# Two value projections of a hybrid decoder layer as one product of seven block products, ahead of the token mixer

## Chip, cores and metric

One Trainium2 chip, one of its cores. The metric is the device time of one execution in microseconds, the median of several runs.

## What is computed

A trunk of two layers on 1024 tokens of 1024 channels. The first layer mixes tokens by gated DeltaNet and short convolutions, the second by HGRN2 (4 heads) and by dilated sliding-window attention (3 dilations, 4 heads); each is followed by a SwiGLU feed-forward part. The change is in the second layer's input projection, whose columns are split into seven parts:

```python
hq, hf, hi, hg, sq, sk, sv = split_cols(h @ w_in, CD_SPLITS)   # 512 x 4, 1536 x 3 columns
o_c = hgrn2_recurrence(heads(silu(hq)), heads(k_in), heads(hi), heads(log_f))
for p, (window, dilation) in enumerate(((128, 1), (512, 4), (2048, 16))):
    o_p, lse_p = dilated_window_attention(sq[:, :, p], sk[:, :, p], sv[:, :, p], window, dilation)
```

`hi` are the values of HGRN2 (512 columns), `sv[:, :, 1]` those of dilation 4 (512 columns). Inside a head, HGRN2 is a recurrence over chunks of the sequence; attention gives an output and a log-sum per dilation, and the three are combined by a softmax.

## The kernel before, in words

Every product of the projections is done in three terms: operands are split into a high and a low half (`split`, line 100: a cast on ScalarE, a subtraction on VectorE), and `mm3` (line 125) sends high x high, high x low and low x high, its three matmuls at lines 135, 136 and 137. A weight unit is 128 x 1024 and has four slots; the raw weights come through a buffer `raw` with two slots and a `spare` with one. PSUM has eight banks: `psu` (3), `psm` (3), `psg` (2).

`Up` (line 288) and its subclass `Local` (line 752) work a pair of projections as one 2 x 2 block product with seven products in place of eight. Its operands are the four quarters of the normalized input, b11 and b21 (first half of the tokens, low and high channels), b12 and b22 (second half), and four combinations t1 to t4 of them. `Local.run` makes queries, keys and HGRN2's inputs this way, f = 0 to 15, and writes them to DRAM. Its instructions on TensorE, VectorE, ScalarE, GpSimd and, from f = 3, the SP queue are in an order written out by hand (`manual_schedule`). In the last pair it loads two weight units for the next stage and takes b12 back from DRAM into the place of t1. In the feed-forward part, `Up.pair` also makes, on VectorE, sums of blocks of the down weights (`block_load`, `block_sums`, lines 457 to 473), 256 columns at a time, and stores them to DRAM.

`mixer_cd` (line 1970) then mixes. Its values are plain products: `v_rows` for HGRN2, two heads (256 columns) at a time, eight token tiles by eight k tiles by three terms; `swa_v(p)` for a dilation, 512 columns. Between groups of their matmuls `tick(cost)` adds credit, rate x cost, to two generators and runs as many of their steps as there is credit for (saved up to 3): `hg_chain`, the recurrence (eight units of head and half, ten steps each, rate 2.2), and `loc`, the attention (three dilations by four heads by four steps, rate 1.6, in the gates 2.5). So value products, and last the gates of HGRN2 (`hgrn_gates`), are what TensorE does while the vector engines work on the two chains. The order is: values of heads 0 and 1, of dilation 4, of heads 2 and 3, of dilation 16, of dilation 1, the gates. The chain may not pass the heads whose values are there (`have_v`). Values of HGRN2 stay in SBUF (`vt`), those of the dilations go through DRAM (`scr_v`). In `mixer_cd` the order on the engines is chosen when the program is built, by the order in which the code issues.

Of the kernel before, what the change touches and what calls it, by code (L numbers as in the profile page):

```python
# [9 lines left out]
F32 = mybir.dt.float32  # L10
# [21 lines left out]
PAIRS = [(None, h) for h in range(4)] + [(p, h) for p in (1, 2, 0) for h in range(4)]  # L32
VGROUPS = ((8, 2), (10, 2), (40, 4), (44, 4), (48, 4))

# [21 lines left out]
def hybrid_trunk_kernel(ctx: ExitStack, tc: tile.TileContext, x_t, w_all, w_down, w_ba, vecs, c_f, c_i, c_rope, out):  # L56
# [97 lines left out]
    hd = [[dr.tile([P, KT, HT], F32, name=f"hd{j}{i}") for i in range(NH)] for j in range(3)]  # L154
    cat = [[dr.tile([KT, P, HT], F32, name=f"cat{i}{j}") for j in range(NH)] for i in range(2)]

    class Trunk:
# [130 lines left out]
    class Up:  # L288
# [168 lines left out]
        def block_load(self):  # L457
            if self.blocks < ND // SB:
                c = slice(self.blocks * SB, (self.blocks + 1) * SB)
                a = self.right.tile([P, 4, SB], F32, tag="sd", name="sd", bufs=1)  # L460
                dma(a, w_down[self.layer].rearrange("x y p n -> p (x y) n")[:, :, c])
                self.block = c, a
                self.blocks += 1

        def block_sums(self):
            if self.block:
                c, a = self.block
                V.tensor_tensor(a[:, 3], a[:, 2], a[:, 3], op=ADD)
                V.tensor_tensor(a[:, 2], a[:, 0], a[:, 2], op=SUB)
                V.tensor_tensor(a[:, 0], a[:, 3], a[:, 0], op=SUB)  # L470
                V.tensor_tensor(a[:, 1], a[:, 1], a[:, 0], op=SUB)
                dma(self.sums_d.rearrange("s p n -> p s n")[:, :, c], a)
                self.block = None
# [20 lines left out]
        def pair(self, f, b11, b21, b22, t1, t2, t3, t4):  # L494

            n = f + 1
            self.p1(f, b11)
            self.add22(f - 1)
# [27 lines left out]
            self.end12(f - 1, b22)  # L526
            if f in (5, 7, 9, 11):
                self.block_sums()
# [3 lines left out]
            self.p6(f, t2)  # L532
            if f in (5, 7, 9, 11):
                self.block_load()
# [217 lines left out]
    class Local(Up):  # L752
# [185 lines left out]
        def run(self, tr, row, b11, b21, hx, close, left, right):  # L938
# [7 lines left out]
            with tc.manual_schedule(engines=engines | {E.SP}):  # L946
                last = len(PAIRS) - 1
                for f in range(3, last + 1):
                    self.pair(f, f == last, b11, b21, b22, t1, t2, t3, t4)
                self.copy22(last)  # L950
                self.add22(last)
                self.end21(last, t4)
                self.rope22(last)
                split(self.lead_w[1][:, 0, :], self.lead_w[1][:, 1, :], self.lead_raw)
                for i, raw in enumerate(self.back):
                    c = slice(2 * i, 2 * i + 2)
                    split(t1[0][:, c, :], t1[1][:, c, :], raw.rearrange("p (k t) -> p k t", k=2))
                self.end12(last, b22)
                self.rope21(last)
                self.add12(last)  # L960
                self.rope12(last)
                while self.adds or self.stores:
                    self.flush()
            return [t1, b22], self.lead_w

        def pair(self, f, last, b11, b21, b22, t1, t2, t3, t4):
# [6 lines left out]
            if not last:  # L973
                an = self.raw("g", n, n % 3 == 1)
            else:
                raws = [self.left.tile([P, DM], F32, tag="spare", name="raw", bufs=1),
                        ring.tile([P, DM], F32, tag="raw", name="raw", bufs=2)]
                for raw, j in zip(raws, (8, 9)):
                    dma(raw, w_all[W_AT["cd", j]])
            self.add22(f - 1)  # L980
# [26 lines left out]
            if last:  # L1007
                self.lead_w = [unit(), unit()]
                split(self.lead_w[0][:, 0, :], self.lead_w[0][:, 1, :], raws[0])
                self.lead_raw = raws[1]  # L1010
            self.rope12(f - 1)
            if not last:
                self.s = self.sums(an, bn)
                self.a, self.b = an, bn
            else:
                self.back = [ring.tile([P, DM], F32, tag="raw", name="raw", bufs=2) for _ in range(2)]
                for i, raw in enumerate(self.back):
                    dma(raw.rearrange("p (k t) -> p k t", k=2), self.b12[:, 2 * i:2 * i + 2, :])
            if f == 3:
# [950 lines left out]
    def mixer_cd(hn, hp, qkd, wv):  # L1970
        catd = cat[1]
        scr_v = dr.tile([3, T_LEN, HT], F32, name="scr_v")
        scr_o = dr.tile([4, 2, T_LEN, 132], F32, name="scr_o")
# [3 lines left out]
        with ExitStack() as es:  # L1977
# [9 lines left out]

            def v_rows(w, tick, dst, tts=range(8)):

                v = [u.rearrange("p z (k e) -> p z k e", k=KH) for u in w]  # L1990
                for tt in tts:
                    half, j = divmod(tt, 4)
                    o = psu()
                    t = slice(j * P, (j + 1) * P)
                    mm3(o[:, 0:256], [(hk(hn[half], 0, k)[:, t], hk(hn[half], 1, k)[:, t], v[k // KH][:, 0, k % KH],
                                       v[k // KH][:, 1, k % KH]) for k in range(KT)])
                    dst(tt, o[:, 0:256])
                    tick(0.5)

            wp = es.enter_context(pool("swa", side="right"))
            attn = hl("attn", (4, P))
            G.memset(attn, 0.0)
            st, carry = hl("st", (3, P)), hl("carry", (P,))
            vts, raws = {}, {}

            def hgrn_v(pair, w, tick, tts=range(8)):
                def put(tt, o):
                    half, j = divmod(tt, 4)  # L2010
                    if j == 0:
                        while pair and half and done_c[0] < 3:
                            next(hg_chain)
                        vts[pair, half] = hl("vt", (4, 256), 3)
                    S.copy(vts[pair, half][:, j, :], o)
                v_rows(w, tick, put, tts)

            def hgrn_vw(pair):
                return wload(("cd", 8 + pair * 2), ("cd", 9 + pair * 2))

# [5 lines left out]
            def hgrn_fq(h, half):  # L2026
                raws[h, half] = [hl(n, bufs=2) for n in ("b", "kk", "q")]
                for i, z in zip((2, 3, 1), raws[h, half]):
                    dma(z, qkd[None, h][i, :, half * HT:(half + 1) * HT])

            def hgrn(h, half, states):
                if half + h == 0:
                    hgrn_fq(0, 0)
                b, kk, q = raws.pop((h, half))
                if h * 2 + half < 7:
# [90 lines left out]
                yield  # L2126
                vt = vts[h // 2, half]
                hv = slice(h % 2 * P, h % 2 * P + P)
                last = half == NH - 1
                o = psg()  # L2130
                for c in range(4 - last):
                    T.matmul(o[:, c * P:(c + 1) * P], kt[:, c, :], vt[:, c, hv], start=True, stop=True)
                before = [states.get(h)] + [st[:, c, :] for c in range(3)]
# [12 lines left out]
                for c in range(4):  # L2146
                    T.matmul(po[:, c * P:(c + 1) * P], attn[:, c, :], vt[:, c, hv],
                             start=True, stop=before[c] is None)
# [37 lines left out]

            def swa_v(p, tick):


                w = wload(*(("cd", 40 + p * 4 + i) for i in range(4)))  # L2190
                v = [u.rearrange("p z (k e) -> p z k e", k=2) for u in w]
# [220 lines left out]

            done_c, have_v, diag = [0], [0], []
            gate_store = [None]
# [4 lines left out]
            def chain():  # L2419
                states = {}  # L2420
                for u in range(8):
                    h, half = divmod(u, 2)
                    while have_v[0] <= h // 2:
                        yield
                    yield from hgrn(h, half, states)
# [34 lines left out]
            hg_chain, loc = chain(), local()  # L2460
            credit, rate = [0.0, 0.0], [2.2, 1.6]

            def tick(cost):

                live = have_v[0] * 4 > done_c[0], bool(wanted or heads or busy[0])
                for i in range(2):
                    credit[i] = min(credit[i] + rate[i] * cost, 3.0 if live[i] else 1.0)
                while credit[0] >= 1 and have_v[0] * 4 > done_c[0]:
                    credit[0] -= 1
                    next(hg_chain, None)  # L2470
# [6 lines left out]

            hgrn_v(0, wv, tick, range(4))
            have_v[0] = 1
            hgrn_v(0, wv, tick, range(4, 8))  # L2480
            swa_v(1, tick)
            attend(1)
            w1 = hgrn_vw(1)
            hgrn_v(1, w1, tick, range(4))
            have_v[0] = 2
            hgrn_v(1, w1, tick, range(4, 8))
            swa_v(2, tick)
            attend(2)
# [270 lines left out]
```

## Time and profile before

| | us |
|---|---|
| median of three runs (2511.23 to 2512.3) | 2511.42 |
| the profiled execution | 2512.06 |
| its span | 2509.5 |
| busy: TensorE, VectorE, ScalarE, GpSimd | 2495.7, 1671.8, 1097.2, 626.7 |

The span is from the first to the last instruction of the profiled execution; some 2.6 us of the device time lie around it. Busy times are unions of the instructions of one engine. Matmuls overlap, so the time beside one of them is longer than the distance to the next. In the second mixer the stages are: 1416 to 1448 us the values of heads 0 and 1 (and the rest of the last pair), to 1503 us those of dilation 4, to 1545 us those of heads 2 and 3, to 1617 us those of dilation 16, to 1687 us those of dilation 1, to 1777 us the gates. "DVE" is VectorE, "ACT" ScalarE, "POOL" GpSimd, "PE" TensorE, "SP" the queue that issues the transfers.

### The profile page before, as it was taken

What the parts mean: (1) busy time and instruction counts of PE and PEld (TensorE: products, weight loads), DVE (VectorE), ACT (ScalarE), POOL (GpSimd) and SP (SyncE); (2) the same over time, 40 slices, a digit from 0 to 9 for tenths busy, and PEclk for the clock granted to TensorE, in tenths of its full rate; (3) what the DMA queues carried; (4) which work ended last, traced back from release to release, by engine and by line L of the source; (5) the groups of instructions that cost most, each with busy time, mean ns of one, the idle gap of its engine ahead of it and who ended that gap; (6) DMA issues with size and microseconds to landing.
All of it is one profiled execution on the core that took longest, in us unless ns stands there. A gap on an engine that the chain in (4) does not pass through costs nothing. (4 is left out here: it accounts for less than half of the span.)

```text
span 2509.5 us, 37550 instructions
## 1 busy us (share of the span) xinstructions
PE 2495.7 (99%) x13955; PEld 2077.6 (83%) x13955; DVE 1671.8 (67%) x2773; ACT 1097.2 (44%) x1934; POOL 626.7 (25%) x591
## 2 busy tenths in 40 slices
PE   9999999999999999999999999999999999999998
PEld 7888888888888888888888889888888888888887
DVE  8987775675556565567788766566668555666654
ACT  5432134343333344444676545556544333334442
POOL 1321111323333300031566410000132333330001
PEclk9999999999999999999999999999999999999999
DMA  4535458334556588644344544577733555668753
GB/s 156 164 122 168 137 164 271 102 113 168 185 193 217 202 295 287 198 139 135 129 147 139 172 147 142 157 203 224 257 118 101 186 181 185 217 202 304 266 177 126
DMA packets 281454, 451.48 MB, mean 180 GB/s; under 512 B 49176, under 2 KB 137784, under 8 KB 281016
## 3 DMA queue, kind: packets, MB, share of 16 engines
q1 hardware_dynamic: 280984, 448.57, 54.6%
q8 instruction: 109, 1.79, 0.3%
q10 hardware_dynamic: 288, 0.52, 0.1%
q14 instruction: 73, 0.60, 0.1%
HBM read 304.74 MB, written 144.26 MB: 179 GB/s over the span
## 5 line engine op out<-in xcount | busy, mean ns | idle before, releaser
L103 DVE TENSOR_TENSOR w<-raw,w 128x1024 fp32r<-128x1024 f32 (+1 forms) x327 | 388.2, 1189 | 141.5 <-ACT w L102 140.6
L102 ACT CAST w<-raw 128x1024 fp32r<-128x1024 f32 (+1 forms) x327 | 309.5, 952 | 286.0 <-PE psu L137 145.9
L135 PE MATMUL psu<-hnh,w 128*128 128x512 f32 x772 | 308.5, 400 | 0.0
L137 PE MATMUL psu<-hnh,w 128*128 128x512 f32 x772 | 301.3, 390 | 0.0
L136 PE MATMUL psu<-hnl,w 128*128 128x512 f32 x772 | 301.2, 390 | 0.0
L196 POOL TENSOR_TENSOR acc<-acc,sq 128x512 f32<-128x512 f32 x52 | 78.2, 1504 | 441.3 <-ACT sq L192 441.2
L335 POOL TENSOR_TENSOR ws<-raw 128x512 f32<-128x512 f32 x54 | 70.2, 1299 | 431.8 <-DMA raw<-in_dram 256.5
L135 PEld LDWEIGHTS psu<-hnh,w 128*128 128x128 f32 x772 | 145.1, 188 | 30.8 <-ACT sq L192 0.8
L137 PEld LDWEIGHTS psu<-hnh,w 128*128 128x128 f32 x772 | 144.9, 188 | 30.9
L136 PEld LDWEIGHTS psu<-hnl,w 128*128 128x128 f32 x772 | 145.2, 188 | 28.3
L103 DVE TENSOR_TENSOR w<-ws,w 128x1024 fp32r<-128x1024 f32 x51 | 70.1, 1374 | 117.2 <-ACT w L102 117.2
L103 DVE TENSOR_TENSOR hidq<-hr,hidq 128x1024 fp32r<-128x1024 f32 x72 | 82.3, 1144 | 77.8 <-ACT hidq L102 77.6
L102 ACT CAST hidq<-hr 128x1024 fp32r<-128x1024 f32 x72 | 70.2, 979 | 103.8 <-DMA hr<-ts 63.0
L135 PE MATMUL psm<-hidq,w 128*128 128x512 f32 (+1 forms) x275 | 106.1, 386 | 0.0
L136 PE MATMUL psm<-hidq,w 128*128 128x512 f32 (+1 forms) x275 | 105.8, 385 | 0.0
L137 PE MATMUL psm<-hidq,w 128*128 128x512 f32 (+1 forms) x275 | 105.8, 385 | 0.0
L426 POOL TENSOR_TENSOR hid<-hid,c 128x512 f32<-128x512 f32 x44 | 62.0, 1408 | 170.5 <-ACT hid L425 170.4
L341 POOL TENSOR_TENSOR raw<-raw,ws 128x512 f32<-128x512 f32 x51 | 78.7, 1543 | 60.4 <-DVE w L103 53.0
L135 PE MATMUL psu<-t4h,w 128*128 128x512 f32 x240 | 93.5, 390 | 0.0
L137 PE MATMUL psu<-t4h,w 128*128 128x512 f32 x240 | 93.4, 389 | 0.0
L136 PE MATMUL psu<-t4l,w 128*128 128x512 f32 x240 | 93.4, 389 | 0.0
L135 PE MATMUL psu<-t3h,w 128*128 128x512 f32 x240 | 93.4, 389 | 0.0
(544 smaller groups left out, 6716.1 us busy)
## 6 DMA issues: line engine op xcount, KB each, us to landing
raw<-in_dram SPq DMA_DIRECT2D x225, 512.0 KB, 4.2
sd<-in_dram SPq DMA_DIRECT2D x44, 512.0 KB, 4.2
hid<-hid SPq DMA_DIRECT2D x88, 256.0 KB, 3.1
sd<-sd SPq DMA_DIRECT2D x44, 512.0 KB, 3.3
hr<-ts SPq DMA_DIRECT2D x40, 512.0 KB, 4.4
raw<-sd SPq DMA_DIRECT2D x40, 512.0 KB, 4.5
qk<-z SPq DMA_DIRECT2D x52, 256.0 KB, 3.9
hd<-h SPq DMA_DIRECT2D x48, 256.0 KB, 2.8
```

Of the source, the lines that this page charges most:

```text
L102: S.copy(hi, src)
L103: eng.tensor_tensor(lo, src, hi.bitcast(F32), op=SUB)
L135: T.matmul(o, lh, rh, start=first and i == 0, stop=False, **kw)
L136: T.matmul(o, lh, rl, start=False, stop=False, **kw)
L137: T.matmul(o, ll, rh, start=False, stop=last and i == n - 1, **kw)
L196: (eng or G).tensor_tensor(a, a, q, op=ADD)
L335: G.tensor_tensor(s[:, HT:], b[:, :HT], b[:, HT:], op=ADD)
L341: G.tensor_tensor(a[:, HT:], a[:, HT:], s[:, :HT], op=SUB)
L426: G.tensor_tensor(h, h, self.c22.pop(f), op=MULT)
```

## The change

HGRN2's and dilation 4's values become the left and right half of one 1024 x 1024 by 1024 x 1024 product, done in seven block products on the operands that `Local` has, in a new stage `rows` at the end of its hand-written order:

- `rows` sends 336 matmuls of 512 columns. Four banks `x` are carried through the products of b11, t2, t3 and t4; products of b21, t1 and b22 go to `psm` and are added on VectorE. Results go to DRAM: `scr_v[1]` for dilation 4, a new `scr_v[3]` for HGRN2.
- Its weights are 14 units, two for each product, requested three ahead (`v_ask`) and split (`v_unit`); two more units are for dilation 16. Six are blocks of the weights as they are, eight are sums of four blocks, laid into `vsum` in DRAM.
- These sums are made by eight more steps of `block_load` and `block_sums`, in the pairs of the first layer's feed-forward part: pairs 4 to 15 have two such steps each, where pairs 5, 7, 9 and 11 had.
- b12 is taken back into t1 at the end of `rows`.
- `mixer_cd` has no value products of HGRN2 and of dilation 4. A unit of the chain loads its values (128 x 4 x 128) with its other inputs. Attention of dilation 4 and the chain begin at once, beside the values of dilation 16. The rates are 3.5 and 2.0.

```diff
+VSETS = (8, 10, 44, 46)
+VGROUPS = ((8, 4), (40, 4), (44, 4), (48, 4))
...
         def block_load(self):
+            n = self.blocks - ND // SB
+            if n < (0 if self.layer else 2 * DM // SB):
                 a = self.right.tile([P, 4, SB], F32, tag="sd", name="sd", bufs=1)
...
+                    i, c = n // (DM // SB), slice(n % (DM // SB) * SB, (n % (DM // SB) + 1) * SB)
+                    for j, at in enumerate(VSETS):
+                        dma(a[:, j], w_all[W_AT["cd", at + i]][:, c])
+                    d = vsum[:, i].rearrange("s p n -> p s n")[:, :, c]
...
+            more = (5, 7, 9, 11) if self.layer else range(4, 16)
...
-            if f in (5, 7, 9, 11):
+            if f in more:
                 self.block_sums()
...
+        def v_ask(self):
...
+                blk = (8, 10, 0, 2, 3, 1, 46)[i // 2]
+                src = w_all[W_AT["cd", blk + k]] if blk >= 8 else vsum[blk, k]
...
+        def rows(self, last, b11, b21, b22, t1, t2, t3, t4):
+
+            def prod(o, i, q, j, ks=range(KH), first=False, end=False):
+                t = slice(j * P, (j + 1) * P)
+                mm3(o, [(q[0][:, k, t], q[1][:, k, t], self.vu[i + k // 2][:, 0, k % 2], self.vu[i + k // 2][:, 1, k % 2])
+                        for k in ks], first, end, skip_group_check=True)
...
+            for j in range(4):
+                y.append(psm())
+                prod(y[j], 2, b21, j, first=True, end=True)
+                g.append(zt())
+                S.copy(g[j], x[j])
+                if j > 1:
+                    self.v_unit()
+                    self.v_ask()
+                V.tensor_tensor(g[j], g[j], y[j], op=ADD)
+                store(3, 0, j, g[j])
...
+            for a in (0, 2):
+                z = []
+                for j in (a, a + 1):
+                    z.append(psm())
+                    prod(z[-1], 8, t1, j, first=True)
+                    c = late(j)
+                    V.tensor_tensor(c, c, z[-1], op=ADD)
+                    store(1, 1, j, c)
+                if a == 0:
+                    self.v_unit()
+                    self.v_unit()
+                    self.v_ask()
+                    self.v_ask()
...
+                for i, j in enumerate((a, a + 1)):
+                    prod(z[i], 10, b22, j, end=True)
+                    V.tensor_tensor(u2[j], u2[j], z[i], op=ADD)
+                    store(3, 1, j, u2[j])
+            for j in range(4):
+                prod(x[j], 12, t4, j, end=True)
...
+                vt = hl("vt", (4, P), 2)
+                dma(vt, scr_v[3, half * HT:(half + 1) * HT, h * P:(h + 1) * P].rearrange("(c p) d -> p c d", p=P))
...
-            credit, rate = [0.0, 0.0], [2.2, 1.6]
+            credit, rate = [0.0, 0.0], [3.5, 2.0]
...
-            hgrn_v(0, wv, tick, range(4))
-            have_v[0] = 1
-            hgrn_v(0, wv, tick, range(4, 8))
-            swa_v(1, tick)
             attend(1)
-            w1 = hgrn_vw(1)
-            hgrn_v(1, w1, tick, range(4))
-            have_v[0] = 2
-            hgrn_v(1, w1, tick, range(4, 8))
-            swa_v(2, tick)
+            next(hg_chain)
+            swa_v(2, tick, wv)
             attend(2)
             swa_v(0, tick)
             attend(0)
```

## Rows read from the trace of the kernel before

**Rows 1.** The page, span and busy time of the engines over the whole run.

```profile
span 2509.5 us, 37550 instructions
...
PE 2495.7 (99%) x13955; PEld 2077.6 (83%) x13955; DVE 1671.8 (67%) x2773; ACT 1097.2 (44%) x1934; POOL 626.7 (25%) x591
```

**Rows 2.** Busy time per engine in five stages, 1423 to 1777 us.

```profile
core 0: us, PE busy (x) PEld busy (x) DVE busy (x) ACT busy (x) POOL busy (x), PEclk, DMA share, GB/s
1423.00:1448.00 25.00, 24.65 (x384) 24.14 (x384) 20.88 (x47) 14.94 (x27) 4.20 (x6) 1.00 0.82 285
1448.00:1503.00 55.00, 55.00 (x561) 45.48 (x550) 31.47 (x75) 20.47 (x42) 5.74 (x11) 1.00 0.37 122
...
1545.00:1617.00 72.00, 71.72 (x676) 60.89 (x676) 38.56 (x123) 34.21 (x91) 5.94 (x11) 1.00 0.58 159
1617.00:1687.00 70.00, 68.09 (x820) 56.61 (x807) 44.27 (x168) 37.42 (x117) 6.20 (x12) 1.00 0.68 191
1687.00:1777.00 90.00, 89.38 (x723) 76.39 (x722) 66.20 (x256) 65.83 (x204) 2.15 (x5) 1.00 0.72 220
```

**Rows 3.** What PE waited for, 1423 to 1778 us, the longest.

```profile
PE psm L2309 <- ACT sc L2304: 1.3, 1, 1.3
```

**Rows 4.** Timeline of PE: start us, us, first and last of two unbroken runs.

```profile
1400.01 0.39 PE L135 MATMUL psm<-hnh,w 128*128 128x512 f32 x1
...
1416.10 0.39 PE L137 MATMUL psu<-t3h,w 128*128 128x512 f32 x1
1416.33 0.28 PE L135 MATMUL psu<-w,hnh 128*128 128x256 f32 x1
...
1422.91 0.28 PE L135 MATMUL psu<-w,hnh 128*128 128x256 f32 x1
...
1430.70 0.28 PE L137 MATMUL psu<-w,hnl 128*128 128x256 f32 x1
```

**Rows 5.** Timeline of PE where the output projection begins.

```profile
1778.32 0.47 PE L135 MATMUL psg<-hnh,w 128*128 128x512 f32 x1
```

**Rows 6.** Groups by line and form, PE, 1416.2 to 1778 us.

```profile
L135 PE MATMUL psu<-w,hnh 128*128 128x512 f32 x96 | 39.0, 406 | 0.3 <-ACT sw L2200 0.3
...
L135 PE MATMUL psu<-w,hnh 128*128 128x256 f32 x64 | 18.6, 291 | 0.3 <-ACT vt L2015 0.3
```

**Rows 7.** Groups by line and form, VectorE and ScalarE, 1423 to 1778 us.

```profile
L103 DVE TENSOR_TENSOR w<-raw,w 128x1024 fp32r<-128x1024 f32 x21 | 25.6, 1219 | 6.8 <-ACT w L102 6.7
L102 ACT CAST w<-raw 128x1024 fp32r<-128x1024 f32 x22 | 23.0, 1047 | 23.4 <-PE psu L137 21.3 <-DMA raw<-in_dram 2.1
...
L2200 ACT COPY sw<-psu 128x512 f32<-128x512 f32 x24 | 14.1, 585 | 31.6 <-PE psu L137 21.2 <-issue 5.8 <-PE psm L2326 1.8
...
L2051 DVE TENSOR_TENSOR m<-m,kk 128x256 f32<-128x256 f32 x32 | 13.4, 419 | 7.6 <-ACT m L2050 7.5
```

**Rows 8.** Timeline of VectorE, one 128x512 addition out of PSUM.

```profile
1417.65 0.68 DVE L884 TENSOR_TENSOR psm<-c,psg 128x512 f32<-128x512 f32 x1
```

**Rows 9.** DMA issues by tile, 1416 to 1778 us: count, KB, us to landing.

```profile
raw<-in_dram SPq DMA_DIRECT2D x23, 512.0 KB, 4.8
```

**Rows 10.** Groups by line, VectorE, 500 to 900 us: block sums.

```profile
L469 DVE TENSOR_TENSOR sd<-sd 128x256 f32<-128x256 f32 x22 | 13.7, 624 | 0.8
...
L471 DVE TENSOR_TENSOR sd<-sd 128x256 f32<-128x256 f32 x22 | 12.4, 563 | 0.8
L470 DVE TENSOR_TENSOR sd<-sd 128x256 f32<-128x256 f32 x22 | 12.3, 557 | 0.8
L468 DVE TENSOR_TENSOR sd<-sd 128x256 f32<-128x256 f32 x22 | 10.4, 472 | 7.7 <-issue 3.6 <-DMA sd<-in_dram 3.0 <-DVE w L103 1.0
```

**Rows 11.** Busy time per engine in the first up stage, columns as above.

```profile
500.00:600.00 100.00, 100.00 (x443) 82.81 (x442) 73.12 (x87) 43.32 (x58) 29.79 (x21) 1.00 0.40 133
```

**Rows 12.** Busy time per engine in two short stretches of the second mixer.

```profile
1500.00:1510.00 10.00, 10.00 (x190) 9.19 (x189) 9.74 (x29) 7.43 (x16) 0.70 (x1) 1.00 0.51 161
1660.00:1670.00 10.00, 9.72 (x158) 8.03 (x155) 9.70 (x45) 8.81 (x32) 1.10 (x3) 1.00 0.78 200
```

## What the change was predicted to do, before it was run

> **What bounds the kernel now.** I read four views. The page comes first: TensorE is busy for 2495.7 of the 2509.5 us, VectorE for 67% [rows 1]. Busy is not the same as at its peak, so next come the stages around the change. The granted clock is 1.00 throughout, the 2.4 GHz level, so no part of the sum is a clock. VectorE is at 31.47 of 55.0 us in one stage and at 66.20 of 90.0 us in the last; TensorE has hardly a hole [rows 2]. The list of waits agrees: the longest wait that TensorE shows in the whole second mixer is 1.3 us [rows 3]. Last, the timeline, for what a matmul really takes. The duration printed beside a 128x512 matmul (0.39 us) overlaps the next one, so I take the distance of starts. From 1400.01 to 1416.10 us there are 72 of them one after another, 16.09 / 71 = 0.2266 us each. From 1422.91 to 1430.70 us there are 66 of 256 columns, 7.79 / 65 = 0.1198 us each [rows 4]. Half the columns cost 0.53 of the time, so columns are what is paid for, and the way to shorten this stretch is to send fewer of them. The stretch runs from the first value matmul at 1416.33 us to the first of the output projection at 1778.32 us [rows 4, 5]: 362.0 us.
>
> **Removed.** HGRN2's values are 384 matmuls of 256 columns (L135 has 64 + 32 + 32 of them, L136 and L137 as many), 384 x 0.1198 = 46.0 us. The values of dilation 4 are a third of the 576 of 512 columns that the three dilations send (96 + 48 + 48 for each of three lines) [rows 6]: 192 x 0.2266 = 43.5 us. Together 89.5 us.
>
> **Added.** Seven products of four token tiles by four k tiles by three terms: 336 matmuls of 512 columns, 336 x 0.2266 = 76.1 us. The balance on TensorE is 13.4 us down. That is 1/8 of the columns with the 256-column overhead on top.
>
> **Waits in the new value stage.** Fourteen weight units are cast (1.05 us, ScalarE) and subtracted (1.22 us, VectorE) [rows 7], where eight were. Two units feed one product of 10.9 us, so cast and subtraction fit four times over. A unit's transfer lands in 4.8 us [rows 9] and is asked for three units ahead. Slots of units (four) and accumulators (four of the eight banks, held through the stage) follow the order by hand. I walked that order: at one place the low half of a unit stands on VectorE behind an addition that itself waits for TensorE. Unit 10 follows the addition for tile 1 of the t1 product, and the b22 product needs unit 10 at once. That is one 0.68 us addition [rows 8] plus one 1.22 us subtraction, 1.9 us. At the hand-over to the second mixer, units 14 and 15 arrive behind the reload of t1; I allow 0.5 us. Sum 2.4 us. Bounds: 0, if matmuls of the next stage fill the holes, and 14 x (1.05 + 1.22) = 32 us, if every unit stood in the path. I stay near the low end because the second mixer's first matmul at 1416.33 us ran ahead of the last pair's remaining products [rows 4], so holes do get filled. The reload of t1, which stood in the last pair, moves to the end of this stage with its two transfers and two splits; TensorE needs t1 next only for the fifth token tile. HGRN2's values come back from DRAM by eight loads of 256 KB, each requested a unit (27 us or more) ahead, and dilation 4's are first read in the third step of attention: 0 for both, with the transfers' landing as their price if that cover went. On the SP queue, stores of z and c stand ahead of later requests and wait for the additions that make them; those additions are at most 5.4 us behind, with three units already requested. The stage moves about 12 MB in 79 us, 152 GB/s; the stage at 1423 us moved 285 GB/s beside full TensorE work [rows 2].
>
> **Block sums in the first up stage.** Eight more sets of four VectorE operations, 0.472 + 0.624 + 0.557 + 0.563 = 2.2 us a set [rows 10], 17.7 us in all, and 8 MB of transfers. Four pairs already carry two sets each, and in the window from 500 us, which holds two such pairs, VectorE is at 73.12, TensorE at 100.00 [rows 11]. A pair is 84 matmuls, 19.0 us, so VectorE has some 5 us free in it. I cost this at 0; the cover is the pair's own matmuls, and without it the price is 17.7 us.
>
> These operations have two SBUF sources, as has L2051; it takes 0.419 us [rows 7] beside a GpSimd that is nearly idle, they take up to 0.624 us [rows 10] beside one that is 30% busy [rows 11]. So the two engines do slow each other here. The Trainium skill, "SBUF — State Buffer", section "Who interferes with whom", says that a VectorE instruction with two SBUF inputs and a GpSimd instruction that reads SBUF exclude each other; this trace agrees in the longer durations, and the page's rule makes the weight sums on GpSimd later as well. By it the first up stage could pay; this is the fourth rival.
>
> **What is left, packed tighter.** This is the term that decides. The second mixer keeps its vector work but has 89.5 us less of matmuls to lay it beside: 362.0 - 89.5 = 272.5 us, less 24 matmuls of the last pair (5.4 us), is 267 us. The HGRN2 chain has eight units of ten steps. In the stage from 1448 us it runs alone with the values: VectorE 31.47 less four subtractions (4.9) is 26.6 us for 8 ticks x 2.2 = 17.6 steps, 1.51 us a step. TensorE: 55.0 - 43.5 = 11.5 us, 0.65 us a step. ScalarE: 20.47 less four casts and eight copies of 0.585 us (8.9) is 11.6 us, 0.66 us a step [rows 2, 7]. Before, the chain is live for 2 + 8 + 4 + 8 + 8 = 30 ticks ahead of the gates, 66 steps, with 1 of saved credit and 4 forced by the buffers of values: 71 of 80. After, a tick of 0.75 gives 2 or 3 steps and one of 1 is cut at 3, so 26 in each of two value loops and 1 ahead: 53. The gates therefore carry 27 steps in place of 9. Their stage (90.0 us now) becomes 90.0 + 18 x 0.65 = 101.7 us for TensorE, 66.2 + 18 x 1.51 = 93.4 us for VectorE and 65.8 + 18 x 0.66 = 77.7 us for ScalarE. VectorE's share goes from 74% to 92%. A value loop gets 26 - 17.6 = 8.4 steps more, 12.7 us of VectorE and 5.5 us of TensorE: that of dilation 1 goes from 44.27 of 70 to 57 of 75.5 us, that of dilation 16 from 38.56 of 72 to 51 us of more than 77 [rows 2].
>
> What does a share of 92% cost TensorE? No stage shows one. The near end: two stretches of 10 us have VectorE at 9.74 and 9.70 with TensorE at 10.00 and 9.72 [rows 12]; at 97%, 93.4 us of work needs 96 us, less than 101.7: cost 0. The far end: the gates stage never does better than its present 74%, 93.4 / 0.74 = 126.2 us: cost 24.5 us. In between, the densest long stage (20.88 of 25 us, 83.5%) [rows 2] gives 111.9 us: cost 10.2 us. I take 4.0 us, a share of 88%, nearer to the short stretches: there TensorE was full while VectorE was, and a busy VectorE with a backlog is just what this stage has.
>
> **Sum.** -13.4 + 2.4 + 0 + 4.0 = -7.0 us. The profiled execution took 2512.06 us (its span of 2509.5 and 2.6 around it), so 2505.1; the median of the runs is 0.6 lower, which gives **2504.4 us**. A change of 0.2%, 5.0 us, is about what a measurement of this kernel can tell from none.
>
> **The rivals.** First, *the vector engines eat it*: the gates stage reaches 80 to 87%, and of the 13.4 us at most 5.0 are left or lost. At 83.5% the sum is -13.4 + 2.4 + 10.2 = -0.8, 2510.6 us. For it: the attention chain passes from TensorE to VectorE to ScalarE and back for every block, and ScalarE is at 76% too. Against it: rows 3 and 12. Second, *the gates stage becomes VectorE's, slower than before*: the HGRN2 steps that are left over meet the combining of the three dilations, and the share stays near 74%: -13.4 + 2.4 + 24.5 = +13.5, 2524.9 us. It decides as soon as the stage takes over 117.7 us, that is below 79%. For it: no stage of 40 us or more in rows 2 is above 74%. Against it: none of these stages was limited by VectorE. Third, *the packing is free* (cost 0 in both new terms): 2511.4 - 13.4 = 2498.0 us; it lies within the forecast's side. Fourth, *the first up stage pays* for its 17.7 us of block sums: -7.0 + 17.7 = +10.7, 2522.1 us. It would need VectorE over 100% in a pair, against [rows 11]. That the change sends as many columns as before can be excluded from the diff: 336 x 512 against 384 x 256 + 192 x 512.
>
> **Chances.** Forecast, with the third rival, 0.47. First rival 0.30. Second 0.20, fourth 0.03. So faster by over 0.2% has 0.47, within it 0.30, slower 0.23. The likeliest case alone lies between 2498.0 and 2506.4. The range has to reach further: its low end is 2498, where every unknown cost is 0 (0.04 is left out below), its high end 2521, a gates stage of 122 us, 76% (0.10 left out above).
>
> **What would show it.** Right: 336 matmuls in 77 to 80 us ahead of the second mixer with one wait near 2 us on VectorE's L103; from their end to the output projection 267 to 275 us; a gates stage of 101 to 108 us with VectorE near 90%; the first up stage still at 100.00. Wrong: a gates stage over 110 us with TensorE waiting for lines of the combining or of the HGRN2 chain; several waits on weights in the value stage; a TensorE hole between 400 and 900 us. I would also be wrong if the HGRN2 steps were drawn into the value stage, whose vector engines are half idle; then the gain would go beyond 13.4 less the two costs.

## The result, and the profile after

The changed kernel takes 2524.11 us, the median of four runs (2520.78 to 2526.62), against 2511.49 us for the kernel before on the same chip: a ratio of 1.0049, interval 1.0031 to 1.0066. Forecast were 2504.4 us, range 2498 to 2521. It is slower by 12.6 us, on the other side and outside the range. The profiled execution took 2526.62 us and its span is 15.0 us longer than in [rows 1].

First the page of the changed kernel, span and busy time, beside [rows 1]:

```profile
span 2524.5 us, 37197 instructions
...
PE 2491.4 (99%) x13715; PEld 2062.4 (82%) x13715; DVE 1695.4 (67%) x2823; ACT 1100.7 (44%) x1932; POOL 637.4 (25%) x591
```

TensorE has 240 instructions fewer and is busy for only 4.3 us less; the span grew, so the loss is time in which TensorE stands, or runs slowly. To find where, I take from TensorE's timeline the first or last matmul of each stage, as in [rows 4, 5]: the last one of the projections, the last two of the value stage, the last of the value loops, the first of the output projection.

```profile
1421.73 0.39 PE L138 MATMUL psu<-t3h,w 128*128 128x512 f32 x1
...
1506.34 0.39 PE L137 MATMUL psg<-w,t4h 128*128 128x512 f32 x1
1506.57 0.39 PE L138 MATMUL psg<-w,t4l 128*128 128x512 f32 x1
...
1685.91 0.39 PE L138 MATMUL psu<-w,b22l 128*128 128x512 f32 x1
...
1793.82 0.39 PE L136 MATMUL psg<-hnh,w 128*128 128x512 f32 x1
```

| stretch | before | after | forecast |
|---|---|---|---|
| start to the last matmul of the projections | 1416.1 | 1421.7 | 1416.1 |
| value stage (336 matmuls and 24 of the last pair) | | 84.8 | 84.0 |
| the two value loops | | 179.3 | 165.3 |
| gates stage | | 107.9 | 105.7 |
| value matmuls to output projection together | 362.2 | 372.1 | 355.0 |
| output projection to the end | 731.2 | 730.7 | 731.2 |

(Forecast: 360 x 0.2266 + 2.4 = 84.0; the 271 us for the second mixer, 267 + 4.0, less the gates' 105.7 leave 165.3 for the loops.) So the 15.0 us are 5.6 ahead of the value stage and 9.9 after it, less 0.5 behind. Against the forecast, two places are wrong: the first layer's up stage by 5.6 us and the value loops by 14.0.

**The up stage.** Busy time per engine from 700 us (columns as in [rows 2]), first of the kernel before, then of the changed one:

```profile
700.00:900.00 200.00, 200.00 (x884) 165.61 (x883) 121.09 (x160) 71.45 (x100) 62.32 (x48) 1.00 0.64 213
...
700.00:900.00 200.00, 195.61 (x859) 160.69 (x858) 124.37 (x173) 67.68 (x95) 71.56 (x50) 1.00 0.69 231
```

TensorE's timeline of the changed kernel there has two holes of 2 us, both ahead of the t3 product (two starts 0.7 and 0.3 us late, at 745 and 764 us, and one slower step behind each of the four make up the 5.6). The time in brackets is idle time; by the distance of starts the next matmul is up to 0.2 us later still, and where the text gives a wait without its line, it is mostly this longer time. The timelines of the SP queue, VectorE and ScalarE show what came before the second hole, and in the first line what came before the first:

```profile
785.63 0.50 PE L136 MATMUL psu<-t3h,w 128*128 128x512 f32 x1 [1.95 <-ACT u L401]
...
806.79 0.50 PE L136 MATMUL psu<-t3h,w 128*128 128x512 f32 x1 [1.83 <-ACT u L401]
...
776.37 0.43 DVE L479 TENSOR_TENSOR sd<-sd 128x256 f32<-128x256 f32 x1 [5.29 <-DMA raw<-in_dram]
...
778.20 0.38 SPq L483 DMA_DIRECT2D vsum<-sd  x1
...
782.63 1.95 SPq L471 DMA_DIRECT2D sd<-in_dram  x4
...
786.84 0.90 DVE L479 TENSOR_TENSOR sd<-sd 128x256 f32<-128x256 f32 x1 [2.40 <-DMA sd<-in_dram]
...
789.15 0.38 SPq L483 DMA_DIRECT2D vsum<-sd  x1
...
792.19 1.76 SPq L471 DMA_DIRECT2D sd<-in_dram  x4
...
796.94 0.43 DVE L479 TENSOR_TENSOR sd<-sd 128x256 f32<-128x256 f32 x1 [4.35 <-DMA sd<-in_dram]
...
802.79 2.22 DVE L104 TENSOR_TENSOR w<-raw,w 128x1024 fp32r<-128x1024 f32 x1 [1.04 <-ACT w L103]
804.93 0.67 DVE L427 TENSOR_TENSOR hid<-u,psg 128x512 f32<-128x512 f32 x1
...
805.63 0.63 ACT L428 ACTIVATE hid<-hid 128x512 f32<-128x512 f32 x1 [2.88 <-DVE hid L427]
```

The tile of the block sums, `sd`, has one slot. A set's store goes out at 778.20, three stores of combinations stand behind it on SP, and the next load waits on SP until the store has landed: it is issued at 782.63. The list of SP's waits between 774 and 784 us has it:

```profile
SPq L471 <- DMA vsum<-sd: 1.7, 1, 1.7
```

VectorE reaches the sum by its written order and stands 2.4 us for the load. So this set's store is late as well, the next load goes out at 792.19, and VectorE stands 4.35 us for that one. Behind it stand additions and the split of a weight unit, then the addition of L427, for which ScalarE waits 2.88 us; ScalarE's next copy (L401) is what TensorE waits for at 806.79. The first hole has the same chain one pair earlier, from the wait of 5.29 us on. The split has a share in it: it takes 2.22 us here and 1.62 ahead of the first hole, beside GpSimd at work on the weight sums, where it took 1.23 us at 776.88 us in the kernel before. So up to 1.0 and 0.4 us of the two holes may be the two engines slowing each other; that was not separated. Between 740 and 830 us VectorE stands so for 18.2 us, at six sums (in the kernel before, at none):

```profile
DVE sd L479 <- DMA sd<-in_dram: 12.9, 5, 4.4
DVE sd L479 <- DMA raw<-in_dram: 5.3, 1, 5.3
```

Most of the operations take 0.42 us in this stretch, 1.7 us a set, where I had counted 2.2; the waiting I had not counted.

**The value loops.** Waits of over 2 us stand at two places; before, the longest was 1.3 us [rows 3]. The list of waits of the changed kernel, around 1541 us:

```profile
PE psm L2418 <- ACT sc L2375: 2.7, 1, 2.7
ACT sw L2292 <- DMA scr_v<-sw: 2.7, 1, 2.7
```

and around 1630 us:

```profile
DVE ol L2458 <- DMA scr_o<-ol: 6.3, 1, 6.3
...
PE psg L2158 <- DVE m L2150: 2.9, 1, 2.9
```

In place of the 2.7 us of the first list the next matmul starts 2.9 us late, so I call both waits 2.9 us. Read from TensorE's lines back: it waits for ScalarE's exponential (L2375) or VectorE's part of the HGRN2 chain (L2150). That engine stands in its order at a copy into a staging tile, `sw` or `ol`, both with two slots, because the store of an earlier content of that slot hasn't landed. Stores of `sw` take up to 6.4 us here, and the transfers move 256 GB/s from 1500 to 1560 us, 159 GB/s before.

The windows of the changed kernel show a second loss behind each wait (the column behind POOL is the granted clock):

```profile
1541.00:1544.00 3.00, 0.53 (x3) 0.53 (x4) 0.47 (x4) 1.66 (x5) 0.00 (x0) 0.78 0.82 316
1544.00:1547.00 3.00, 3.00 (x11) 2.52 (x11) 1.91 (x6) 2.19 (x7) 0.00 (x0) 0.50 0.30 100
1547.00:1550.00 3.00, 3.00 (x10) 2.33 (x9) 0.00 (x0) 0.00 (x0) 0.00 (x0) 0.58 1.03 293
1550.00:1554.00 4.00, 4.00 (x141) 3.21 (x140) 0.58 (x2) 0.58 (x1) 0.00 (x0) 1.00 0.55 149
...
1629.00:1632.00 3.00, 0.31 (x23) 0.34 (x27) 2.92 (x12) 2.80 (x7) 0.00 (x0) 0.91 0.20 48
1632.00:1636.00 4.00, 2.52 (x57) 1.86 (x49) 4.00 (x12) 2.53 (x5) 0.00 (x0) 0.50 0.35 132
1636.00:1639.00 3.00, 3.00 (x38) 2.76 (x38) 1.88 (x5) 2.48 (x9) 1.69 (x4) 0.62 0.82 240
```

After each wait the clock is at 0.50, the 1.2 GHz level, for several microseconds; the mean over 1540:1560 and over 1620:1640 is 0.83, that is at most 0.17 x 20 = 3.4 us lost in each, less what of it falls into idle time. A wait of 2.9 us thus costs up to some 6, and near 1545 us TensorE counts as busy all through the second part of that, so a list of waits shows only the first.

**The value stage and the gates** went as forecast. In the value stage one wait of 1.8 us stands at the foreseen place:

```profile
PE psm L137 <- DVE w L104: 1.8, 1, 1.8
```

and in the gates VectorE is at 77.86 of 90 us, 87%, where 88% had been taken:

```profile
1700.00:1790.00 90.00, 86.27 (x929) 74.37 (x927) 77.86 (x277) 67.46 (x199) 8.33 (x14) 1.00 0.63 198
```

### The profile page after: what moved, and what is told of

Its sections match the earlier page's. It is cut to its first block, busy times and chain, and to the rows that moved or that the text cites. A ratio compares the mean times of both kernels' runs of the same rounds, so it can differ in the third digit from the quotient of the medians.

```text
span 2524.5 us, 37197 instructions
## 1 busy us (share of the span) xinstructions
PE 2491.4 (99%) x13715; PEld 2062.4 (82%) x13715; DVE 1695.4 (67%) x2823; ACT 1100.7 (44%) x1932; POOL 637.4 (25%) x591
## 5 line engine op out<-in xcount | busy, mean ns | idle before, releaser
L104 DVE TENSOR_TENSOR w<-raw,w 128x1024 fp32r<-128x1024 f32 (+1 forms) x333 | 400.4, 1205 | 155.0 <-ACT w L103 153.5
L103 ACT CAST w<-raw 128x1024 fp32r<-128x1024 f32 (+1 forms) x333 | 315.3, 954 | 280.6 <-PE psu L138 126.2
L381 ACT ACTIVATE gt<-gt 128x512 f32<-128x512 f32 x44 | 27.8, 632 | 155.2 <-DVE gt L378 155.2
L136 PE MATMUL psu<-t4h,w 128*128 128x512 f32 x240 | 93.5, 390 | 0.8 <-ACT c L890 0.8
L137 PE MATMUL psu<-t3l,w 128*128 128x512 f32 x240 | 93.4, 389 | 0.0
```

Source lines behind the costliest of these rows:

```text
L103: S.copy(hi, src)
L104: eng.tensor_tensor(lo, src, hi.bitcast(F32), op=SUB)
L136: T.matmul(o, lh, rh, start=first and i == 0, stop=False, **kw)
L137: T.matmul(o, lh, rl, start=False, stop=False, **kw)
L381: S.activation(self.g1[f], self.g1[f], AF.Silu)
```

## The experiments

The theory: two separate losses, each a wait for a transfer by an engine that keeps an order. The late block-sum loads cost 5.6 us in the up stage; the two staging tiles with two slots cost the waits in the value loops and the low clock behind them. The kernel before was timed again beside each experiment, at 2511.5 to 2512.7 us, so the ratios compare better than the medians. The rivals: the loops are simply packed too densely (rates 3.5 and 2.0); or the waits depend on the moment at which the mixer is entered. A question inside the theory is whether SP's order or the transfers themselves make the stores late. Stretches in all runs are read from TensorE's timeline, as above.

| kernel | median | ratio to before, interval | projections end | value stage | loops | gates | rest |
|---|---|---|---|---|---|---|---|
| changed | 2524.11 | 1.0049, 1.0031 to 1.0066 | 1421.7 | 84.8 | 179.3 | 107.9 | 730.7 |
| 1 no sums | 2515.64 | 1.0015, 1.0006 to 1.0024 | 1415.9 | 84.8 | 172.6 | 107.6 | 730.9 |
| 2 sums moved | 2518.44 | 1.0021, 1.0011 to 1.0030 | 1416.6 | 84.8 | 177.0 | 107.6 | 730.8 |
| 3 three slots | 2513.05 | 1.0007, 0.9998 to 1.0016 | 1420.3 | 84.9 | 167.1 | 107.7 | 731.0 |
| 4 rates of before | 2526.95 | 1.0061, 1.0047 to 1.0075 | 1421.2 | 84.8 | 143.4 | 135.7 | 740.4 |
| 5 = 2 + 3 | 2510.76 | 0.9992, 0.9983 to 1.0001 | 1416.3 | 84.8 | 169.4 | 107.7 | 730.7 |
| 6 = 5, units early | 2507.26 | 0.9980, 0.9971 to 0.9989 | 1416.2 | 82.7 | 166.5 | 107.6 | 730.9 |
| 7 `ol` alone | 2521.26 | 1.0031, 1.0020 to 1.0043 | 1420.8 | 84.8 | 172.4 | 107.6 | 730.8 |
| 8 stores by POOL | 2523.18 | 1.0041, 1.0027 to 1.0054 | 1420.2 | 84.8 | 177.6 | 107.7 | 730.9 |
| 9 `sw` alone | 2518.89 | 1.0034, 1.0022 to 1.0046 | 1419.5 | 84.8 | 172.1 | 107.7 | 730.7 |
| 10 = 6, rates 2.8, 1.8 | 2516.65 | 1.0019, 1.0010 to 1.0028 | 1416.4 | 82.8 | 158.9 | 121.8 | 735.2 |

### 1. No block sums in the first layer

```diff
-            more = (5, 7, 9, 11) if self.layer else range(4, 16)
+            more = (5, 7, 9, 11)
...
-            if n < (0 if self.layer else 2 * DM // SB):
+            if n < 0:
...
-                src = w_all[W_AT["cd", blk + k]] if blk >= 8 else vsum[blk, k]
+                src = w_all[W_AT["cd", (blk if blk >= 8 else 44) + k]]
```

This kernel leaves out the sums of the value weights; the products that need them take a plain block in their place.

> The changed kernel without its eight extra block-sum steps in the first up stage; the two products that need the sums take plain weight blocks of the same size instead, so their values are not computed. Theory A (the extra steps cost the 5.6 us by which the last pair of the second mixer's projections ends later, 1416.1 to 1421.7 us): that end comes back to 1416 us and the total falls by 5 to 6 us, to about 2518.5. Rival (the sums are free, the 5.6 us come from elsewhere): no change, 2524.

The projections end at 1415.9 us: the 5.6 us are the sums' doing, all of them. The loops fell too, from 179.3 to 172.6 us, though no sum is made there. So the waits in the loops move with small shifts in time; waits of 1.2 to 1.4 us (idle time) are left where 2.9 stood, and one fall of the clock.

### 2. The sums in other pairs

```diff
-            more = (5, 7, 9, 11) if self.layer else range(4, 16)
+            more = (5, 7, 9, 11) if self.layer else (*range(4, 13), 14, 17, 19)
```

> The changed kernel with the second block-sum step in pairs 4 to 12, 14, 17 and 19 in place of 4 to 15. Theory A with its detail (only pairs that also reload and combine t2 and t3 have no room; the waits stood at 744, 783 and 804 us): some of the three waits go and up to two new ones come, total 2519 to 2525. If it is the mere number of steps that counts, 2524.

All sums are made; the second steps of pairs 13 and 15 have gone to 17 and 19, so that from pair 13 on no two neighbours carry two. The projections end at 1416.6 us. Busy time from 700 us in this kernel:

```profile
700.00:900.00 200.00, 200.00 (x884) 165.62 (x883) 128.37 (x176) 70.60 (x99) 67.08 (x49) 1.00 0.71 236
```

VectorE does more in this window than in the changed kernel and TensorE has no hole (700 to 900 us). From 740 to 830 us VectorE stands 6.0 us for the loads of `sd`, where it stood 18.2:

```profile
DVE sd L479 <- DMA sd<-in_dram: 3.6, 2, 2.9
DVE sd L479 <- DMA raw<-in_dram: 2.4, 1, 2.4
```

The total, 2518.44 us, lies 0.6 below the span expected. So it was not VectorE's work as such, but sets that, from pair 13 on, came closer together than one slot of `sd` is stored and loaded again there. That the slot is the reason is read from the waits; a second slot for `sd` was not tried.

### 3. Three slots for the staging tiles

```diff
-                    vs = tl("sw", bufs=2)
+                    vs = tl("sw", bufs=3)
...
-                    ol = tl("ol", (4, 132), 2)
+                    ol = tl("ol", (4, 132), 3)
...
-                go = tl("sw", bufs=2)
+                go = tl("sw", bufs=3)
```

> The changed kernel with three slots in place of two for the tiles by which values and attention outputs leave for DRAM (sw and ol). Theory B (in the two value loops ScalarE and VectorE stand behind a store that has not landed, TensorE then waits 2.9 us at 1541 and at 1629 us and its clock falls to half for some 7 us twice): both waits and both clock drops go, the second mixer falls from 287 to about 275 us, total about 2512. Rival (the chain steps are simply issued too densely for the vector engines): the waits move, at most 3 us less, 2521 or more.

The loops take 167.1 us, 12.2 less. The two waits (2.9 + 2.9) and the two stretches at low clock (3.4 + 3.4 at most) came to 12.6 at most. The same stretches in this kernel, granted clock 1.00:

```profile
1540.00:1560.00 20.00, 19.71 (x310) 16.33 (x309) 13.01 (x46) 11.03 (x32) 1.93 (x5) 1.00 0.74 220
1620.00:1640.00 20.00, 18.05 (x211) 14.82 (x210) 13.01 (x55) 10.97 (x39) 2.48 (x5) 1.00 0.79 217
```

### 4. The rates of the kernel before

```diff
-            credit, rate = [0.0, 0.0], [3.5, 2.0]
+            credit, rate = [0.0, 0.0], [2.2, 1.6]
```

> The changed kernel with the rates of before, 2.2 and 1.6. By the density theory the two value loops lose their waits and fall from 179 to about 157 us, but some 44 steps of HGRN2 are left for the gates, VectorE needs about 119 us there and the gates take 125 to 135 us: total within 5 us of 2524. By theory B the waits in the loops get rarer as far as fewer attention outputs meet the stores, with the same lengthening of the gates: 2522 to 2530.

The loops shrink to 143.4 us, below the 157 expected, but the steps left over make the gates 135.7 us, and the rest takes 9.7 more. Busy time in this kernel's gates:

```profile
1690.00:1780.00 90.00, 81.46 (x1100) 67.18 (x1097) 82.52 (x285) 64.28 (x180) 14.45 (x21) 1.00 0.54 168
```

VectorE is at 92% and TensorE loses a tenth. Density is needed in the loops; thinner packing is no way out.

### 5. Sums moved and three slots

Edits 2 and 3 together.

> Edits of the second and third experiment together: block sums in pairs 4 to 12, 14, 17, 19; tiles `sw` and `ol` of the second mixer with three slots. If the two losses are separate (theory), their gains add: the third experiment's median of 2513.05, less what its first up stage still lost against the second's (end of the last projection pair 1420.26 against 1416.55): 2509.3; worked from the changed kernel, 2524.1 - 11.1 - 5.7 = 2507.3. So 2507 to 2510, faster than the kernel before by 2.5 to 5 us; end of the last projection pair 1416 to 1417, second mixer 273 to 276 us, granted clock 1.00 in both loops over the value units. Rival (the second mixer depends on when it is entered, so that three slots only happened to suit the old moment): second mixer 279 us or more with a wait of over 2 us on a store, total 2513 or more.

2510.76 us, 0.8 more than the upper end of the theory's span, and not told from the kernel before. Both losses went, but a wait of 1.9 us showed near 1509 us, TensorE's first chain step behind a GpSimd operation of the recurrence, with the clock at 0.91 in 1500:1520; the loops take 169.4 us and not 167.1. So the rival has a share: what the mixer meets on entry varies by some 2 us.

### 6. The same, with two weight units split earlier

```diff
             for a in (0, 2):
                 z = []
+                if a == 0:
+                    self.v_unit()
+                    self.v_unit()
+                    self.v_ask()
+                    self.v_ask()
                 for j in (a, a + 1):
...
-                if a == 0:
-                    self.v_unit()
-                    self.v_unit()
-                    self.v_ask()
-                    self.v_ask()
-                else:
+                if a:
                     self.v_unit()
                     self.v_unit()
```

> The fifth experiment, and in the value stage the splits of value units 10 and 11 ahead of the two additions at L104's place, not behind them. Theory (the wait of 1.9 us there is VectorE's order: the units' splits stand behind additions that wait for TensorE's own products): the wait goes, the value stage falls from 84.8 us to 83.0, total 1.5 to 2 us below the fifth experiment. Rival (the units wait for their loads, and VectorE standing there holds up the additions too): the value stage stays at 84.5 us or more, total the same within 0.7 us or longer.

The value stage falls by 2.1 us as expected; the total falls by 3.5, since the wait of 1.9 us on entry went as well and the loops are back at 166.5 us. Its span is 2504.0 us. Windows of this kernel over the value stage and the loops:

```profile
1421.00:1499.00 78.00, 78.00 (x346) 64.59 (x345) 30.17 (x34) 25.84 (x34) 3.72 (x6) 1.00 0.48 166
1500.00:1560.00 60.00, 58.93 (x728) 48.74 (x727) 44.60 (x146) 35.82 (x96) 6.53 (x12) 1.00 0.81 256
1560.00:1620.00 60.00, 58.98 (x795) 49.84 (x793) 44.20 (x162) 35.82 (x103) 6.16 (x12) 1.00 0.80 201
1620.00:1680.00 60.00, 58.01 (x772) 48.30 (x772) 46.08 (x169) 37.33 (x116) 6.38 (x12) 1.00 0.75 209
```

TensorE has no hole in the value stage and the clock is 1.00 throughout. This version beats both kernels: 0.2% faster than the one before, interval 0.1 to 0.3%.

### 7 and 9. One tile at a time

In 7 only the line of `ol` of edit 3, in 9 only its line of `vs`.

> Three slots for `ol` alone, all else as in the changed kernel. Theory (each of the two long waits has its own staging tile): the wait of 2.9 us near 1629 us, which VectorE passes on from the store of `ol`, goes together with the fall of the granted clock in 1620:1640 to 0.83; the one of 2.9 us near 1541 us, behind the store of `sw`, stays, with the clock of 0.83 in 1540:1560. Half of the third experiment's gain: 2518 to 2520. Rival (one of the two starts the other, the earlier one being the start): both stay, 2523 or more; or (the `ol` store alone counts) both go, 2514.

> Three slots for `sw` alone, all else as in the changed kernel. With `ol` alone at three, the wait near 1541 us came down from 2.87 to 1.66 us and the one near 1628 us from 2.93 to 2.06 us, the latter now behind the store of `sw`. If each tile causes its own part (theory), here the wait near 1541 us goes wholly, and near 1628 us one of 2 to 3 us stays, which VectorE passes on from the store of `ol`, with a fall of the clock there: second mixer 279 to 282 us against 287.3, total 2518 to 2521. Rival (`sw`, the earlier one, starts both): both go, second mixer 275 to 276 us, total 2514 to 2516.

With `ol` alone at three, the wait near 1541 us stays in part, 1.5 us, and the clock stays at 1.00 behind it; near 1628 us one of 2.0 us is left, with VectorE no longer at a store of `ol`, and the clock is at 0.91 in that stretch. The waits of this kernel from 1538 and from 1618 us:

```profile
ACT sw L2292 <- DMA scr_v<-sw: 1.5, 1, 1.5
...
ACT sw L2292 <- DMA scr_v<-sw: 2.1, 1, 2.1
...
PE psg L2225 <- ACT e L2220: 2.0, 1, 2.0
```

With `sw` alone, no wait of 0.9 us or more is left near 1541 us, and near 1621 us the other one stands, 2.1 us, the clock at 0.83 behind it, as waits and windows of this kernel show:

```profile
DVE ol L2458 <- DMA scr_o<-ol: 5.5, 1, 5.5
...
PE psg L2158 <- DVE m L2150: 2.1, 1, 2.1
```

```profile
1620.00:1640.00 20.00, 16.41 (x167) 14.17 (x163) 13.03 (x57) 12.98 (x44) 1.47 (x4) 0.83 0.60 171
```

Neither tile starts the other's wait. The one near 1541 us is behind `sw`; the one near 1628 us is behind `ol`, and with that gone a shorter one behind `sw` shows there. The gains in the loops, 6.9 and 7.2 us, make 14.1 where both together gave 12.2. Experiment 9 came out in the theory's span, 279.8 us for the second mixer and 2518.89 in all; experiment 7's total lay 1.3 us above what the theory expected: its up stage lost 4.7 us again, as little as the tiles have to do with it.

### 8. The stores issued by another engine

```diff
-                    dma(scr_v[p, tt * P:(tt + 1) * P, :], vs)
+                    G.dma_start(scr_v[p, tt * P:(tt + 1) * P, :], vs)
...
-                            dma(d4[:, b, 2 * g:2 * g + 2, 0:w], o4[:, b, :, 0:w])
+                            G.dma_start(d4[:, b, 2 * g:2 * g + 2, 0:w], o4[:, b, :, 0:w])
...
-                            dma(d4[e, :, 4 * g:4 * g + 4, 0:w], ol[e * 64:(e + 1) * 64, :, 0:w])
+                            G.dma_start(d4[e, :, 4 * g:4 * g + 4, 0:w], ol[e * 64:(e + 1) * 64, :, 0:w])
```

> Two slots as in the changed kernel, but the stores of `sw` (values of the three attention dilations) and of `ol` are issued by POOL and not by SP. Theory (SP takes its transfers in order, and these stores stand behind loads that wait for their tiles or fill the queue ahead of them, so that the slots come free late): both waits of 2.9 us fall below 1 us, the granted clock stays at 1.00 in both loops, the second mixer takes 275 to 278 us, total 2513 to 2516. Rival (the 16 DMA engines are so busy, 0.9 of some stretches, that a store lands after 6 us whoever issues it; or POOL, in order itself, issues them late): waits of over 2 us stay, the second mixer takes 284 us or more, total 2521 or more.

My theory of SP's order fell: 2523.18 us, loops 177.6. Issued by GpSimd, the stores of `sw` take 2.3 to 6.4 us to land (2.0 to 6.4 from SP), and the waits of this kernel from 1534 and from 1620 us are

```profile
ACT sw L2292 <- DMA scr_v<-sw: 4.7, 1, 4.7
...
DVE ol L2458 <- DMA scr_o<-ol: 3.5, 1, 3.5
...
ACT sw L2292 <- DMA scr_v<-sw: 1.8, 1, 1.8
```

For `sw` it is the landing that is long, whoever issues it. For `ol` the wait fell from 6.3 to 3.5 us, so a part of that one may be SP's order; TensorE's waits there are then 1.5 and 1.7 us in place of one of 2.9, near 1541 us 2.2 us are left, and the clock still falls behind both places (0.91 over 20 us): 1.7 us are gained in the loops. What makes a landing long (the 16 DMA engines' load, or the other loads under way) was not separated.

### 10. Thinner packing on the best version

```diff
-            credit, rate = [0.0, 0.0], [3.5, 2.0]
+            credit, rate = [0.0, 0.0], [2.8, 1.8]
```

> The sixth experiment with the rates at which HGRN2's steps are laid beside the value units at 2.8 and 1.8, between those of the kernel before (2.2, 1.6) and of the changed kernel (3.5, 2.0). Theory (with three slots the value loops bear the dense packing, TensorE being busy for 98% of them and more, so that thinner packing only moves steps to a stage whose own attention covers them no better): second mixer 274 to 276 us against 274.1, total within 1.5 us of 2507.3 or longer. Rival (the dense packing still costs in the loops): loops shorter than 174 us with no more in the gates stage, total under 2505.5.

9.4 us longer than experiment 6: the loops give 7.6 us, the gates take 14.2 and the rest 4.3. With three slots the loops do bear the rates of the change.

## Why the prediction was wrong, point by point

- **Pace and balance of the matmuls: right.** 360 matmuls and one wait make 84.8 us; without the wait 82.7 (experiment 6), 360 x 0.2266 = 81.6. The matmuls cost what they were to cost.
- **Waits in the value stage, 2.4 us: right, 0.8 us too low (84.8 - 81.6 = 3.2).** The wait behind the addition for tile 1 was put at 1.9 us and its matmul starts 1.9 us late. What is left of the 84.8, 1.3 us, is mostly one wait of 1.0 us ahead of the last pair's t4 product, which I hadn't foreseen; the hand-over had been given 0.5.
- **Block sums, "I cost this at 0": the first step that failed.** It measured 5.6 us. I compared VectorE's busy share with the room in a pair, which held: VectorE had the room. What I left out is that each set waits for a load into the one slot that the set before must first leave, with VectorE's additions queued behind. The window that I read [rows 11] is of an earlier stretch, in which pairs with two sets have a pair with one between them; after the change twelve such pairs are neighbours, the last of them beside the loads and stores of the down projection's combinations. The fourth rival had the place, at 0.03, but another cause and price: it wanted VectorE over 100%. The two engines slowing each other is at most a part of it: 1.0 and 0.4 us in the two holes, and experiment 2 makes every sum, GpSimd being busy for 67.08 of 200 us, and loses 0.5 us. By the Trainium skill, "SBUF — State Buffer", section "Who interferes with whom", a VectorE instruction with two SBUF inputs contends with a GpSimd instruction that reads SBUF; the split of 2.22 us agrees, and in experiment 2 TensorE shows no hole from it between 700 and 900 us.
- **Packing, 4.0 us: the step that failed most.** From the end of the value stage to the output projection it is 287.2 us, so the term measured 287.2 - 267 = 20.2 us. The gates, where I put it, were right: 107.9 us for 105.7 at 87% of VectorE. The loops, which I took to pack freely at 57 of 75.5 us, are 14.0 us over. Not by VectorE's share: with three slots, the same packing takes 167.1 us, 1.8 over. I looked for the cost on the engines' busy shares and not at what the denser order does to buffers. It is not that more goes through the tiles: from 1506 to 1686 us `sw` is stored 15 times and `ol` 28 times, before 15 and 26. But the stores land later, those of `sw` from 1506 to 1596 us in 5.9 us (median) for 3.2 before, beside more transfers, and two slots are no longer enough. I priced dilation 4's and HGRN2's values from DRAM by who reads them, and not by the traffic they add; whether that traffic is what makes the stores land late no run shows.
- **The clock: not in the sum at all.** It read 1.00 in all of [rows 2], so I kept it at 1.00. It about doubled the price of the two waits.
- **The first rival** (vector engines eat it) had the gates' share, 80 to 87%, at its upper end, and with it a cost of 107.9 - 101.7 = 6.2 us there for my 4.0; but that is not where the time went. **The second** (the gates become VectorE's, 2524.9 us) is wrong as a mechanism. It comes within 0.8 us of the result by accident: its gates stage of 126 us took 107.9. Experiments 4 and 10 have stages as long as it describes, 135.7 and 121.8 us, in experiment 4 with VectorE at 92% and not 74%.
- **The third rival**, free packing at 2498.0, was too low as well: the best version, with both losses removed, takes 2507.3, 2.9 us above my forecast.
- **What was to show it wrong** did: a TensorE hole between 400 and 900 us, at 784 and 805 us.

## What to carry to other kernels

Before you cost an added step at nothing because its engine has room, find the load it waits for and see what stands behind it in that engine's order: sets of 2.2 us that fit still stopped TensorE twice for 2 us. When work is packed closer, count the slots of every staging tile against the time that its store takes to land, not just the busy shares: here one more slot for two tiles gave 11 us. Then check the clock behind every long wait, since here it cost up to as much again.

## What the runs showed of the hardware

The clock was the surprise. In the changed kernel the granted clock fell to 0.50 after the waits of 2.9 us, and stayed at 1.00 after those of 2.1 and 2.0 us in the up stage and of 1.9 us in the value stage. In experiment 3 a wait of 2.1 us in the up stage, at 802 us, did have a fall behind it:

```profile
803.00:806.00 3.00, 2.23 (x7) 1.76 (x8) 1.31 (x1) 2.60 (x4) 2.58 (x3) 0.73 0.12 44
806.00:809.00 3.00, 3.00 (x11) 2.41 (x10) 1.79 (x2) 0.59 (x2) 0.00 (x0) 0.70 0.75 252
```

Two waits of the same length thus cost 2.1 us in one kernel and some 3.8 in another (0.27 and 0.30 of 3 us more). That may be a part of the spread of the changed kernel's runs, 5.8 us; it was not tested.
